# Queue order in a two-layer hybrid decoder trunk: first transfers on two queues, splits, exponentials and one value product moved

## The chip, the core and the metric

The kernel runs on one core of one Trainium2 chip. A core has five engines that work side by side, each through its own queue of instructions in order: TensorE (PE in the profile; PEld is its weight load), VectorE (DVE), ScalarE (ACT), GpSimd (POOL) and SyncE (SP, which here only issues transfers). The metric is the device time of one execution in microseconds (us); lower is better.

## The reference, cut to what matters

Two layers; x is 512 tokens by 1024, all in float32. Each layer is a half-step SwiGLU network, a mixer with three groups of heads, a second half-step SwiGLU network and a norm.

```python
for l in range(DEPTH):                                        # 2 layers
    h = x + 0.5 * swiglu(rms_norm(x, ffn1_norm[l]), ...)      # D 1024, FF 2816
    n = rms_norm(h, mix_norm[l])
    p = n @ w_in[l]
    u_conv, q, k, v, q_mem = jnp.split(p, splits, axis=-1)
    y_conv = conv_module(u_conv, ...)     # GLU, causal depthwise conv of 31 taps on 384 channels, LayerNorm, swish
    q = apply_rope(rms_norm(q.reshape(B, S, 6, 64), swa_q_norm[l]), cos, sin)
    k = apply_rope(rms_norm(k.reshape(B, S, 2, 64), swa_k_norm[l]), cos, sin)
    y_swa = sliding_window_attention(q, k, v, swa_sinks[l])   # window 128, softmax with a sink per head
    ...
    y_mem = memory_attention(qm, mk, mv)                      # 4 heads on 256 memory tokens
    y = jnp.concatenate([y_conv, y_swa, y_mem], axis=-1)
    h = h + y @ w_out[l]
    h = h + 0.5 * swiglu(rms_norm(h, ffn2_norm[l]), ...)
    x = rms_norm(h, final_norm[l])
```

## The kernel before, in words

The residual stream `h` lies transposed in SBUF as eight blocks d of 128 features by 512 tokens. Every float32 product is made of three passes (`mm3`, L176 to L178): each operand is split into a high and a low part, and high·high, low·high and high·low are added in PSUM. A split of a weight costs ACT one copy (`whi`, L145) and DVE one subtraction (`wlo`, L146). In `split_by_dma` ACT makes both halves (L150, L151), and a DMA that POOL issues adds the weight to the second (L152). `split_scaled` (L155, L156) makes `xhi` and `xlo`, the operand of the next stage, from a block of `h`; the same object adds the squares of the block to the sum for the next norm (`sq`, L236 on ACT; `st`, L248 on DVE), and PE sums that over features (L202).

At the start SP issues every transfer: the gains, half of w1, block 0 of x, half of w3, and the other blocks.

A network (`ffn`) makes its first products plainly and the rest with `up_pair`, a form with seven products in place of eight; each is followed by the products with w2. In the second layer's first network `after()` (L1053) rescales `h` by eight DVE instructions, issued behind the gate of the first `up_pair`.

The mixer follows a list of steps, `ORDER`: `c` is half a convolution projection, `q` queries and keys of one block of 128 tokens, `Q` their transposition, `v` values and memory queries of one block, `V` the transposition of the latter, `g` the scores of one group of heads, `a` attention, `t` taps, `s` the swish and what follows. `queries(0)` splits its four weights into the buffers `ghi` and `glo`. `attention` walks ten groups (`GROUPS`, `r` for memory, `w` for window): exponentials of the scores (L800, into `uu` or `pr`), transposition on PE (L810), copy on ACT (`aux`, L812), product with the values on PE (L821), division by the sums (`scaled`), transposition and split (`attended`). For window heads the sum has a term for the sink: POOL adds it (L791), ACT takes its exponential (`esw`, L829). The output weights are split in `out_weights`: two before the groups and one each at groups 3 and 5.

The 93 taps of the convolution (`taps`, L939) run on DVE as filler. `EARLY` of them are free; the others are tied by `LATER` to the groups: some so many behind each group's maxima (`nmr`, `nmw`).

A scheduler with a model of each engine turns the program into one fixed order per engine; `issue_after` names an instruction behind which another may be placed. It sets an order in the queue and no wait.

Of the kernel before, what the change touches and what calls it, by code (L numbers as in the profile page):

```python
# [13 lines left out]
AF = mybir.ActivationFunctionType  # L14
# [32 lines left out]
ORDER = "c00 c01 q0 c10 q1 c11 Q0 q2 q3 Q1 c20 c21 Q2 v0 v1 V0 Q3 V1 g0 g1 v2 v3 a t0 t1 t2 s"  # L47

EARLY = 49
LATER = (1, 12, 5, 4, 3, 3, 3, 3, 3, 3)  # L50
# [14 lines left out]
def trunk(ctx: ExitStack, tc: tile.TileContext, xT, memT, pos, w1a, w3a, w2a, w1b, w3b, w2b,  # L65
# [44 lines left out]
    nc.sync.dma_start(gn, gains)  # L110
# [4 lines left out]
    for k in range(KD):  # L115
        if k % 4 == 0:
            nc.sync.dma_start(first[0][:, halves[k // 4]], w1a[0, 0, :, halves[k // 4]])
        nc.sync.dma_start(h[:, k, :], xT[:, k, :])
        if k % 4 == 0:
            nc.sync.dma_start(first[1][:, halves[k // 4]], w3a[0, 0, :, halves[k // 4]])  # L120
# [33 lines left out]
    def split_scaled(hi, lo, x, col):  # L154
        A.activation(hi, x, AF.Copy, scale=col)  # L155
        V.scalar_tensor_tensor(out=lo, in0=x, scalar=col, in1=hi.bitcast(F32), op0=ALU.mult, op1=ALU.subtract)  # L156

# [95 lines left out]
    class Next:  # L253
# [5 lines left out]
        def __call__(self, d):  # L259
            split_scaled(self.x[0][:, d, :], self.x[1][:, d, :], h[:, d, :], self.gain[:, d : d + 1])  # L260
            for s, scale in self.stats:
                s.add(h[:, d, :], 1.0 if scale is None else scale[:, d : d + 1])
# [78 lines left out]
    def up_pair(l, w13, f, M):  # L341
# [26 lines left out]
        def add(out, a, b):  # L368
            V.tensor_tensor(out=out, in0=a, in1=b, op=ALU.add)  # L369
# [15 lines left out]
        for i in range(2):  # L385
            w = unit(X[i])
            product(xy[i][:, x0], w, 1, 5)
            A.activation(part[i][:, x0], xy[i][:, x0], AF.Copy)
            product(zv[i][:, x1], w, 0, 7)
            add(to[i][:, :, x1], zv[i].rearrange("p (n t) -> p n t", n=2), part[i][:, x0].unsqueeze(1).to_broadcast([P, 2, QT]))  # L390
# [14 lines left out]
    def ffn(l, w13, w2, x, sums, factors, last, at_product, aside=None):  # L405
# [44 lines left out]
        for q, (f0, nf) in enumerate(QUARTERS):  # L450
            ahead = 2 if q + 1 < len(QUARTERS) else 0
            for f in range(f0, f0 + nf + ahead, 2):
                if f not in g:
                    g[f], g[f + 1] = up_pair(l, w13, f, M)
                    if f == PLAIN:
                        with tc.issue_after(M.gated.ins):
                            after()
# [86 lines left out]

    def head_scale(ps, col, n, out=None):

        sq = tm("hsq", "sq", 2)[:, 0 : n * HD]
        A.activation(sq, ps, AF.Square, scale=col)
# [74 lines left out]
    def mixer(l, x, st, last):  # L623
# [28 lines left out]
        def spare():  # L652

            return tuple(z.rearrange("p i s -> p (i s)") for z in gated_pair())
# [38 lines left out]
        def queries(t):  # L693
            if not t:
                ww["q"] = [weights(wqk[l, i], 1024, G if i else V, spare()) for i in range(4)]
# [30 lines left out]
        def values(t):  # L726
# [9 lines left out]
            head_scale(ps[:, 0:256], rc[:, t : t + 1], NM, rm[:, t, :])  # L736

# [85 lines left out]
        def scaled(kind, b, po):  # L823
# [3 lines left out]
            if kind == "w":  # L827
                e = esw[:, b]
                A.activation(e, e, AF.Exp)  # L829
# [31 lines left out]
        def attention():  # L861
# [18 lines left out]
            for d in range(2):  # L880
                with tc.issue_after(keyed[2].ins):
                    out_weights(d)
            yy.extend([gated_pair() for _ in range(KD // 2)][::-1])
            y.extend(at(p, ALL, i, ALL) for p in yy for i in range(2))
            for n, (kind, *pairs) in enumerate(GROUPS):
# [8 lines left out]
                if n in (3, 5):  # L894
                    with tc.issue_after(raised[GROUPS[n - 1][0], *GROUPS[n - 1][-1]].ins):
                        out_weights(len(out_w))
# [108 lines left out]
    def stages(st, gain):  # L1005
        def factors(r):
            return gain, kept(spread(r), "R"), lambda: None

        return lambda: rms_cols(st, D), factors

    for l in range(L):
# [16 lines left out]
        mixer(l, nxt.x, before, into(gn[:, l, N_FFN2], (st, None)))  # L1028
        sums, factors = stages(st, gn[:, l, N_FFN2])
        st, fin = Stat("st"), gn[:, l, N_FIN]  # L1030
        if l + 1 < L:
# [15 lines left out]
            def factors(r, gg=gg, fin=fin):  # L1047
                R = kept(spread(r[1]), "R")

                def after():  # L1050
                    RF = kept(spread(r[0]), "RL")
                    for d in range(KD):
# [70 lines left out]
```

## Time and profile before

| what | value |
|---|---|
| median of 3 runs | 1791.13 us (1789.97 to 1793.52) |
| profiled execution | 1790.99 us, its span 1789.2 us |
| PE busy | 1757.0 us, 98% |
| DVE, ACT, POOL busy | 71%, 50%, 11% |
| PE idle inside the first 25 us | 6.4 us |
| PE busy from 25 to 300 us | 275 of 275 us |
| PE busy in 400 to 500 us and 1300 to 1400 us | 94.9 of 100 us each |

PE is busy nearly all the time, so the table is read from its few gaps: the start, the two mixers (about 355 to 530 us and 1237 to 1412 us) and the end. A granted clock below 1 in a stretch says that TensorE ran there at its lower level for a part of the time.

### The profile page before, as it was taken

The page shows a single profiled execution, that of the slowest core. Times are in us where ns is not written, and L with a number is a line of the kernel's source. Part 1 is how long each engine was busy: PE and PEld are TensorE (multiplying, and loading weights), DVE is VectorE, ACT ScalarE, POOL GpSimd, SP SyncE. Part 2 cuts the span into 40 slices and gives each one's busy share as a digit, 9 for nine tenths or more (in the row PEclk, how much of TensorE's full clock was granted, in tenths as well). Part 3 has the DMA queues.
Part 4 walks back from the last instruction along what each step waited for, and adds up shares of the span by engine and source line. Part 5 has one row for each costly group of instructions (what it writes and reads, how often), then busy time and mean ns, then how long its engine had stood idle before and what let it go on. Part 6 is the DMA issues. An engine that isn't in the chain of part 4 may idle for free.

```text
span 1789.2 us, 28081 instructions
## 1 busy us (share of the span) xinstructions
PE 1757.0 (98%) x11004; PEld 1581.5 (88%) x11004; DVE 1272.3 (71%) x1887; ACT 899.4 (50%) x1367; POOL 194.4 (11%) x217
## 2 busy tenths in 40 slices
PE   8999999999999999999999999999999999999997
PEld 6989999878788989898889898989787889998986
DVE  6969666589947857575678685756797567666755
ACT  6646444464765535353655453535455655453532
POOL 1001000034221000000010000000441210000000
PEclk9999999999999999999999999999999999999998
DMA  9456555183167547464656474643631966574622
GB/s 280 125 163 177 165 139 145 57 217 70 30 176 172 139 136 177 127 173 128 165 136 170 131 190 135 169 114 105 158 70 30 234 127 171 136 183 119 168 74 82
DMA packets 95892, 253.32 MB, mean 142 GB/s; under 512 B 9872, under 2 KB 14224, under 8 KB 95760
## 3 DMA queue, kind: packets, MB, share of 16 engines
q1 hardware_dynamic: 77040, 190.45, 34.9%
q0 software_dynamic: 18720, 61.09, 19.3%
q8 instruction: 86, 1.41, 0.3%
q14 instruction: 46, 0.38, 0.1%
HBM read 249.40 MB, written 2.10 MB: 141 GB/s over the span
## 4 chain that ended last, share of the span: by engine, by line
PE 81%; issue 6%; DVE 6%; DMA 4%; ACT 3%; POOL 0%; SPq 0%; POOLq 0%; DVEq 0%; ACTq 0%
PE mm L177 12%; PE mm L176 11%; PE mm L178 11%; PE po L176 8%; PE po L178 8%; PE po L177 8%; PE pt L176 6%; PE pt L177 6%; PE pt L178 6%; DVE there L939 2%; DMA glo<-in_wqk 1%; DMA raw<-in_wout 1%; DVE wlo L146 1%; PE cf L178 1%; PE cf L176 1%
## 5 line engine op out<-in xcount | busy, mean ns | idle before, releaser
L145 ACT ACTIVATE whi<-raw 128x1024 fp32r<-128x1024 f32 (+3 forms) x344 | 324.5, 945 | 440.5 <-PE mm L177 223.5
L146 DVE TENSOR_TENSOR wlo<-raw,whi 128x1024 fp32r<-128x1024 f32 (+3 forms) x344 | 372.0, 1083 | 133.9 <-ACT whi L145 132.6
L177 PE MATMUL mm<-glo,whi 128*128 128x512 f32 x752 | 293.3, 390 | 0.8 <-DVE glo L146 0.8
L176 PE MATMUL mm<-ghi,whi 128*128 128x512 f32 x752 | 293.3, 392 | 0.0
L178 PE MATMUL mm<-ghi,wlo 128*128 128x512 f32 x734 | 285.7, 389 | 0.9 <-DVE wlo L146 0.9
L177 PE MATMUL po<-ml,whi 128*128 128x256 f32 x864 | 244.5, 283 | 0.0
L178 PE MATMUL po<-mh,wlo 128*128 128x256 f32 x864 | 244.5, 283 | 0.0
L176 PE MATMUL po<-mh,whi 128*128 128x256 f32 x864 | 244.4, 283 | 0.0
L176 PE MATMUL pt<-xhi,whi 128*128 128x256 f32 x864 | 243.3, 283 | 0.6 <-DVE g L369 0.6
L178 PE MATMUL pt<-xhi,wlo 128*128 128x256 f32 x864 | 243.9, 283 | 0.0
L177 PE MATMUL pt<-xlo,whi 128*128 128x256 f32 x864 | 243.9, 283 | 0.0
L475 DVE SCALAR_TENSOR_TENSOR h<-mm,h 128x512 f32<-128x512 f32 x128 | 87.8, 689 | 133.3 <-PE mm L178 133.3
L177 PEld LDWEIGHTS mm<-glo,whi 128*128 128x128 f32 x752 | 141.3, 188 | 29.9 <-DVE glo L146 1.6
L176 PEld LDWEIGHTS mm<-ghi,whi 128*128 128x128 f32 x752 | 141.3, 188 | 29.4 <-DVE h L475 1.2
L176 PEld LDWEIGHTS pt<-xhi,whi 128*128 128x128 f32 x864 | 165.2, 192 | 1.7 <-DVE g L369 0.8
L177 PEld LDWEIGHTS pt<-xlo,whi 128*128 128x128 f32 x864 | 165.7, 192 | 0.8
L176 PEld LDWEIGHTS po<-mh,whi 128*128 128x128 f32 x864 | 165.8, 192 | 0.7
L177 PEld LDWEIGHTS po<-ml,whi 128*128 128x128 f32 x864 | 165.8, 192 | 0.6
L178 PEld LDWEIGHTS po<-mh,wlo 128*128 128x128 f32 x864 | 165.8, 192 | 0.0
L178 PEld LDWEIGHTS pt<-xhi,wlo 128*128 128x128 f32 x864 | 165.6, 192 | 0.0
L178 PEld LDWEIGHTS mm<-ghi,wlo 128*128 128x128 f32 x734 | 137.8, 188 | 30.2 <-DVE wlo L146 1.3
L939 DVE SCALAR_TENSOR_TENSOR there<-ypad,par,there 128x512 f32<-128x512 f32 x180 | 136.7, 770 | 1.6
(312 smaller groups left out, 3312.9 us busy)
## 6 DMA issues: line engine op xcount, KB each, us to landing
raw<-in_w2a SPq DMA_DIRECT2D x48, 384.0 KB, 3.5
raw<-in_w2b SPq DMA_DIRECT2D x48, 384.0 KB, 3.6
raw<-in_w1b SPq DMA_DIRECT2D x26, 512.0 KB, 3.7
raw<-in_w3b SPq DMA_DIRECT2D x26, 512.0 KB, 4.1
raw<-in_w1a SPq DMA_DIRECT2D x25, 512.0 KB, 3.7
raw<-in_w3a SPq DMA_DIRECT2D x25, 512.0 KB, 3.8
wsum<-in_w1a SPq DMA_DIRECT2D x18, 512.0 KB, 4.5
wsum<-in_w3a SPq DMA_DIRECT2D x18, 512.0 KB, 4.4
```

The source lines that it names most:

```text
L145: A.activation(hi, x, AF.Copy)
L146: on.tensor_tensor(out=lo, in0=x, in1=hi.bitcast(F32), op=ALU.subtract)
L176: T.matmul(ps, a[0], b[0], start=first, stop=False, **more)
L177: T.matmul(ps, a[0], b[1], start=False, stop=False, **more)
L178: tail[0] = T.matmul(ps, a[1], b[0], start=False, stop=last, **more)
L475: added = V.scalar_tensor_tensor(out=h[:, d, :], in0=ps, scalar=0.5, in1=h[:, d, :], op0=ALU.mult, op1=ALU.add)
L939: V.scalar_tensor_tensor(out=cv[:, c, :], in0=ypad[:, c, j : j + S], scalar=conv_w[:, c, j : j + 1], in1=cv[:, c, :], op0=ALU.mult, op1=AL ...
```

## The change

What it does, edit by edit. The gains and blocks 0 and 2 of x are loaded through ACT's queue, the rest through SP's. The splits of three of the four query weights are placed behind the last `xhi` of the stage before. The output weights 0 to 3 are split during `values` (three behind the first block's, one behind the third's) and no longer at the groups. The sinks' exponential is placed behind the last exponential of its block. In `ORDER` the value product `v2` stands in front of the first scores `g0`, and `g0` in front of `V1`. `EARLY` goes from 49 to 55 and `LATER` is shorter at its end. The rescaling of `h` is issued in two halves, behind the gates of two pairs.

```diff
-ORDER = "c00 c01 q0 c10 q1 c11 Q0 q2 q3 Q1 c20 c21 Q2 v0 v1 V0 Q3 V1 g0 g1 v2 v3 a t0 t1 t2 s"
-EARLY = 49
-LATER = (1, 12, 5, 4, 3, 3, 3, 3, 3, 3)
+ORDER = "c00 c01 q0 c10 q1 c11 Q0 q2 q3 Q1 c20 c21 Q2 v0 v1 V0 Q3 v2 g0 V1 g1 v3 a t0 t1 t2 s"
+EARLY = 55
+LATER = (1, 12, 5, 4, 3, 3, 3, 3, 2, 2)
...
-    nc.sync.dma_start(gn, gains)
+    nc.scalar.dma_start(gn, gains)
...
-        nc.sync.dma_start(h[:, k, :], xT[:, k, :])
+        (nc.scalar if k in (0, 2) else nc.sync).dma_start(h[:, k, :], xT[:, k, :])
...
-                    if f == PLAIN:
-                        with tc.issue_after(M.gated.ins):
-                            after()
+                    if f in (PLAIN, PLAIN + 2):
+                        with tc.issue_after((M.gated if f == PLAIN else M.turned).ins):
+                            after(f > PLAIN)
...
-                ww["q"] = [weights(wqk[l, i], 1024, G if i else V, spare()) for i in range(4)]
+                ww["q"] = []
+                for i in range(4):
+
+                    with tc.issue_after(operand.rounded.ins) if i else nullcontext():
+                        ww["q"].append(weights(wqk[l, i], 1024, G if i else V, spare()))
...
+            for d in {0: (0, 1, 2), 2: (3,)}.get(t, ()):
+                with tc.issue_after((squared[-1] if d > 1 else keyed[2]).ins):
+                    out_weights(d)
...
-                A.activation(e, e, AF.Exp)
+                with tc.issue_after(raised[kind, b, CC - 1].ins):
+                    A.activation(e, e, AF.Exp)
...
-            for d in range(2):
-                with tc.issue_after(keyed[2].ins):
-                    out_weights(d)
...
-                if n in (3, 5):
-                    with tc.issue_after(raised[GROUPS[n - 1][0], *GROUPS[n - 1][-1]].ins):
-                        out_weights(len(out_w))
...
+                def after(half):
+                    if not half:
+                        spreads.append(kept(spread(r[0]), "RL"))
+                    RF = spreads[0]
+                    for d in range(4 * half, 4 * half + 4):
```

The first place is ScalarE's queue at the first layer's mixer start; `xhi` are the last blocks of the operand, `sq` their squares, and each `ghi` with its `glo` the two halves of one query weight. Before:

```order
L155 ACTIVATE xhi_3587<-h_79,gn_80 128x512
L236 ACTIVATE sq_3689<-h_79 128x512
L150 ACTIVATE ghi_3847<-raw_3849 128x1024
L151 ACTIVATE glo_3848<-raw_3849 128x1024
L155 ACTIVATE xhi_3587<-h_79,gn_80 128x512
L236 ACTIVATE sq_3714<-h_79 128x512
L150 ACTIVATE ghi_3854<-raw_3856 128x1024
L151 ACTIVATE glo_3855<-raw_3856 128x1024
L155 ACTIVATE xhi_3587<-h_79,gn_80 128x512
L236 ACTIVATE sq_3739<-h_79 128x512
L150 ACTIVATE ghi_3861<-raw_3863 128x1024
```

The same place in the changed kernel, from the same `xhi` (block 5) on:

```order
L155 ACTIVATE xhi_3587<-h_79,gn_80 128x512
L237 ACTIVATE sq_3689<-h_79 128x512
L155 ACTIVATE xhi_3587<-h_79,gn_80 128x512
L237 ACTIVATE sq_3714<-h_79 128x512
L155 ACTIVATE xhi_3587<-h_79,gn_80 128x512
L150 ACTIVATE ghi_3847<-raw_3849 128x1024
L151 ACTIVATE glo_3848<-raw_3849 128x1024
L150 ACTIVATE ghi_3854<-raw_3856 128x1024
L151 ACTIVATE glo_3855<-raw_3856 128x1024
L237 ACTIVATE sq_3739<-h_79 128x512
L150 ACTIVATE ghi_3861<-raw_3863 128x1024
```

The last `xhi` has moved in front of two weights' halves; the last block's square, `sq_3739`, stands behind the same two weights as before.

The second place is ScalarE's queue around the first scores: `here`, `query` and `hsq` from a `po` tile are the reads of a value product, `there` from a `pt` tile is the copy of a transposition `V`, `whi` and `wlo` the halves of an output weight, `uu` the first exponentials. Before:

```order
L583 ACTIVATE there_3743<-pt_4281 128x2x128
L583 ACTIVATE here_3742<-pt_4285 128x3x128
L720 ACTIVATE here_3742<-pt_4285 128x128
L583 ACTIVATE there_3743<-pt_4292 128x2x128
L800 ACT_TABLE_LOAD
L800 ACTIVATE uu_3748<-mm_4296,nmr_3757,rm_3754 128x256
```

In the changed kernel:

```order
L586 ACTIVATE there_3743<-pt_4302 128x2x128
L586 ACTIVATE here_3742<-pt_4306 128x3x128
L728 ACTIVATE here_3742<-pt_4306 128x128
L741 ACTIVATE here_3742<-po_4313,rc_3752 128x2x64
L743 ACTIVATE query_3749<-po_4313,rc_3752 128x256
L551 ACTIVATE hsq_4340<-po_4313,rc_3752 128x256
L150 ACTIVATE whi_4347<-raw_4349 128x640
L151 ACTIVATE wlo_4348<-raw_4349 128x640
L586 ACTIVATE there_3743<-pt_4363 128x2x128
L812 ACT_TABLE_LOAD
L812 ACTIVATE uu_3748<-mm_4354,nmr_3757,rm_3754 128x256
```

Between the two copies `there` (of `V0` and of `V1`) now stand the three reads of `v2` and both halves of an output weight.

The third place is DVE's queue from the second value block's `hv` to the first window maxima; `there<-ypad,par,there` is a tap, `nmr` are the maxima of the memory scores, `nmw` those of the window scores. Before:

```order
L551 TENSOR_SCALAR hv_4277<-hs_4276 128x4
L939 SCALAR_TENSOR_TENSOR there<-ypad,par,there 128x512
L773 TENSOR_REDUCE nmr<-mm 128x2 x2
L774 SCALAR_TENSOR_TENSOR nmr<-nmr,rm 128x4
```

In the changed kernel:

```order
L554 TENSOR_SCALAR hv_4298<-hs_4297 128x4
L946 SCALAR_TENSOR_TENSOR there<-ypad,par,there 128x512 x5
L553 TENSOR_REDUCE hs_4342<-hsq 128x4
L785 TENSOR_REDUCE nmr<-mm 128x2 x2
L946 SCALAR_TENSOR_TENSOR there<-ypad,par,there 128x512
L554 TENSOR_SCALAR hv_4343<-hs_4342 128x4
L786 SCALAR_TENSOR_TENSOR nmr<-nmr,rm 128x4
```

From this `hv` to the instruction that finishes the first window maxima (`nmw<-nmw,nsink 128x6`) the queue has 14 taps before and 18 now; from the next `nmw<-nmw,nsink` to the last of the split parts `glo` before the final block it has 24 before and 22 now.

## Rows read from the trace of the kernel before

**Rows 1.** The page's first part: busy us, share of the span, instructions of each engine.

```profile
PE 1757.0 (98%) x11004; PEld 1581.5 (88%) x11004; DVE 1272.3 (71%) x1887; ACT 899.4 (50%) x1367; POOL 194.4 (11%) x217
```

**Rows 2.** PE's waits over the whole span: releaser, us in total, times, longest.

```profile
PE mm L176 <- ACT xhi L155: 7.5, 3, 6.3
PE po L821 <- ACT aux L812: 3.7, 2, 1.8
...
PE pt L581 <- ACT there L583: 1.6, 2, 0.8
...
PE mm L178 <- DVE wlo L146: 0.9, 1, 0.9
```

**Rows 3.** Timeline of ACT, start: start us, us, instruction, [idle before, releaser].

```profile
4.40 0.63 ACT L145 ACTIVATE whi<-raw 128x512 fp32r<-128x512 f32 x1 [2.17 <-DMA raw<-in_w1a]
5.53 0.72 ACT L155 ACTIVATE xhi<-h,gn 128x512 fp32r<-128x512 f32 x1 [0.50 <-DMA h<-in_xT]
```

**Rows 4.** Windows: stretch, length, busy of each engine, granted clock, DMA share, GB/s.

```profile
3.00:4.00 1.00, 0.00 (x0) 0.00 (x0) 0.00 (x0) 0.00 (x0) 0.00 (x0) 1.00 0.97 242
```

**Rows 5.** Timeline of ACT, first layer, mixer start.

```profile
371.21 1.06 ACT L150 ACTIVATE ghi<-raw 128x1024 fp32r<-128x1024 f32 x1
...
373.12 0.70 ACT L155 ACTIVATE xhi<-h,gn 128x512 fp32r<-128x512 f32 x1
373.73 0.62 ACT L236 ACTIVATE sq<-h 128x512 f32<-128x512 f32 x1
```

**Rows 6.** Timeline of DVE, the same place.

```profile
370.42 0.68 DVE L475 SCALAR_TENSOR_TENSOR h<-mm,h 128x512 f32<-128x512 f32 x1
...
374.53 0.68 DVE L248 TENSOR_TENSOR st<-st,sq 128x512 f32<-128x512 f32 x1
```

**Rows 7.** Timeline of PE, the same place.

```profile
375.27 1.05 PE L202 MATMUL cf<-onesq,st 128*128 128x1 f32 x8
```

**Rows 8.** Timeline of DVE, second layer, mixer start.

```profile
1252.56 0.68 DVE L475 SCALAR_TENSOR_TENSOR h<-mm,h 128x512 f32<-128x512 f32 x1
```

**Rows 9.** Timeline of PE, second layer, mixer start.

```profile
1257.65 1.05 PE L202 MATMUL cf<-onesq,st 128*128 128x1 f32 x8
```

**Rows 10.** Timeline of PE, first layer, from the second transposition V to attention.

```profile
438.04 0.44 PE L581 MATMUL pt<-cst,aux 128*128 128x128 f32 x2 [0.81 <-ACT there L583]
...
440.33 0.45 PE L176 MATMUL po<-ghi,xhi 128*128 128x384 f32 x1
...
448.79 0.60 PE L810 MATMUL pt<-cst,uu 128*128 128x128 f32 x4
```

**Rows 11.** Timeline of ACT, first layer, scores and first groups.

```profile
436.61 0.37 ACT L733 ACTIVATE here<-cf,rc 128x128 f32<-128x128 f32 x1 [3.01 <-PE cf L178]
...
437.59 0.39 ACT L583 ACTIVATE there<-pt 128x256 f32<-128x256 f32 x1
...
454.20 0.81 ACT L800 ACTIVATE uu<-mm,nmw,rq 128x128 f32<-128x128 f32 x2
...
457.44 0.73 ACT L150 ACTIVATE whi<-raw 128x640 fp32r<-128x640 f32 x1
458.07 0.59 ACT L812 ACTIVATE aux<-pt 128x512 f32<-128x512 f32 x1
```

**Rows 12.** Timeline of DVE, the same stretch.

```profile
443.19 3.90 DVE L939 SCALAR_TENSOR_TENSOR there<-ypad,par,there 128x512 f32<-128x512 f32 x5
...
454.00 0.17 DVE L790 TENSOR_TENSOR nmw<-nmw,nsink 128x6 f32<-128x6 f32 x1
```

**Rows 13.** Windows of 5 us with the clock below full, inside the two attentions.

```profile
460.00:465.00 5.00, 5.00 (x28) 3.46 (x27) 3.99 (x8) 2.50 (x8) 0.91 (x2) 0.66 0.74 131
...
1340.00:1345.00 5.00, 3.64 (x17) 3.65 (x18) 4.25 (x10) 4.32 (x11) 1.49 (x2) 0.64 0.41 76
1345.00:1350.00 5.00, 5.00 (x27) 3.37 (x27) 2.94 (x7) 1.43 (x4) 0.29 (x1) 0.68 0.31 55
```

**Rows 14.** Timeline of DVE, second layer's first network: the rescaling of h.

```profile
967.47 5.38 DVE L1053 SCALAR_TENSOR_TENSOR h<-h,gn,RL 128x512 f32<-128x512 f32 x8
```

More of the change, by code (lines that the diff above doesn't have):

```diff
@@ L154, in split_scaled @@
     def split_scaled(hi, lo, x, col):
-        A.activation(hi, x, AF.Copy, scale=col)
+        rounded = A.activation(hi, x, AF.Copy, scale=col)
         V.scalar_tensor_tensor(out=lo, in0=x, scalar=col, in1=hi.bitcast(F32), op0=ALU.mult, op1=ALU.subtract)
+        return rounded
     def pair():
@@ L259, in __call__ @@
         def __call__(self, d):
-            split_scaled(self.x[0][:, d, :], self.x[1][:, d, :], h[:, d, :], self.gain[:, d : d + 1])
+            self.rounded = split_scaled(self.x[0][:, d, :], self.x[1][:, d, :], h[:, d, :], self.gain[:, d : d + 1])
             for s, scale in self.stats:
@@ L368, in add @@
         def add(out, a, b):
-            V.tensor_tensor(out=out, in0=a, in1=b, op=ALU.add)
+            return V.tensor_tensor(out=out, in0=a, in1=b, op=ALU.add)
         for i in range(2):
@@ L389, in up_pair @@
             product(zv[i][:, x1], w, 0, 7)
-            add(to[i][:, :, x1], zv[i].rearrange("p (n t) -> p n t", n=2), part[i][:, x0].unsqueeze(1).to_broadcast([P, 2, QT]))
+            M.turned = add(to[i][:, :, x1], zv[i].rearrange("p (n t) -> p n t", n=2), part[i][:, x0].unsqueeze(1).to_broadcast([P, 2, QT]))
         w = unit(z)
@@ L543, in heads @@
         return x.rearrange("p (h e) -> p h e", e=HD)
+    squared = []
     def head_scale(ps, col, n, out=None):
         sq = tm("hsq", "sq", 2)[:, 0 : n * HD]
-        A.activation(sq, ps, AF.Square, scale=col)
+        squared.append(A.activation(sq, ps, AF.Square, scale=col))
         ss, v = sm(n, f"hs{n}"), sm(n, f"hv{n}")
@@ L621, in prepare, with mixer @@
         memory(l)
-    def mixer(l, x, st, last):
+    def mixer(l, operand, st, last):
+        x = operand.x
         o = CC * TAPS
@@ L1006, in factors @@
         def factors(r):
-            return gain, kept(spread(r), "R"), lambda: None
+            return gain, kept(spread(r), "R"), lambda half: None
         return lambda: rms_cols(st, D), factors
@@ L1027, in trunk @@
         before, st = st, Stat("st")
-        mixer(l, nxt.x, before, into(gn[:, l, N_FFN2], (st, None)))
+        mixer(l, nxt, before, into(gn[:, l, N_FFN2], (st, None)))
         sums, factors = stages(st, gn[:, l, N_FFN2])
@@ L1047, in factors @@
             def factors(r, gg=gg, fin=fin):
[L1048 to L1052, printed above, removed]
+                R, spreads = kept(spread(r[1]), "R"), []
+                def after(half):
[3 more added lines that the diff above has]
+                    for d in range(4 * half, 4 * half + 4):
                         V.scalar_tensor_tensor(out=h[:, d, :], in0=h[:, d, :], scalar=fin[:, d : d + 1], in1=RF, op0=ALU.mult, op1=ALU.mult)
```

## The prediction

> **What bounds the kernel now.** I read the page's first part before anything else: PE is busy for 1757.0 us of a span of 1789.2 [rows 1]. Two things can change the time, then: the 32.2 us in which PE stands, and the clock at which it runs. No edit takes a matmul away, so every term below is a stand of PE that is moved, lengthened or taken away, or a stretch of clock behind one.
>
> Next I read PE's waits [rows 2]. The reader is to see how small each is: 6.3 us for the first `xhi` of the kernel, two more waits for `xhi` that make 1.2 together (7.5 less 6.3; they stand at the two mixer starts), two of 1.8 for `aux` in attention, two of 0.8 for the copy behind a transposition, one of 0.9 for a `wlo`. The edits aim at all of these. Then I read the engines' timelines at those places, to see what the waited-for engine was doing, and last the windows with their granted clock [rows 13]: inside attention, behind the stands for `aux`, the mean clock of 5 us falls to 0.66 in layer 1, and to 0.64 and 0.68 in layer 2, which means TensorE spends much of these windows at 1.2 instead of 2.4 GHz. A window at 0.66 costs (1 − 0.66) × 5 = 1.7 us where PE is busy through it. That is my price for a fall of the clock.
>
> The sum is made against the profiled execution, 1790.99 us (span 1789.20 and 1.79 around it), 0.14 below the median of 1791.13. Its bound for no change is 0.2%, 3.6 us: faster is below 1787.5, slower above 1794.7.
>
> **The start: 0 (−0.7 to +0.9).** ACT splits the first weight at 4.40, waits, and begins `xhi` at 5.53 on the arrival of block 0 of x [rows 3]. The changed kernel sends block 0 through ACT's queue, beside the weights on SP's; but ACT's own order now has both weights' first copies ahead of the first `xhi`. The transfers are no idle resource there: at 3 to 4 us the DMA share is 0.97 at 242 GB/s [rows 4]. If the half of w3 and block 0 land close behind the first weight, `xhi` begins at 4.40 + 0.63 = 5.03 at best behind one copy, or 5.66 behind two less what they overlap: about 0.7 earlier than 5.53 at best. If the second weight lands only where `xhi` now stands, one copy of 0.63 and a small delay go in front of it: +0.9. I take 0, between the ends, as the load on the transfers is as large as before.
>
> The row of the DMA share is one place where the Trainium skill speaks against the edit: "Trainium Kernel Development and Optimization", section Key Constraints, says that transfers from SP's, ACT's and POOL's queues share the same 16 DMA engines, and that a second queue saves only issue time. The trace agrees so far as the share of 0.97 goes; by that rule this term would be at most the issue time, and the sum stays as it is.
>
> **The rescaling in halves: −1.05 (−1.1 to 0).** In layer 2's first network eight DVE instructions take 5.38 us in a row [rows 14], and a `wlo` that stands behind them holds PE for 0.9 [rows 2]. In halves only four stand there, 2.7 us, so the `wlo` comes 2.7 earlier, more than the 0.9 needed. I add 0.15 for the slower first matmul behind a wait. The second half must find 2.7 us on DVE one pair later, where DVE (71% busy over the span [rows 1]) waits for PE; without that room the 0.9 comes back there, hence the end at 0.
>
> **The mixer's start: +3.4 (0 to +4).** This is the term that I trust most. Before, ACT runs a weight's halves, `xhi`, `sq`, the next weight's halves, `xhi` and the last `sq`. The pair of halves takes 1.91 (371.21 to 373.12), `xhi` 0.61 to the next start, and the last `sq` begins at 373.73 [rows 5]; the last `st` follows on DVE at 374.53 [rows 6] and PE's sum over features at 375.27 [rows 7], 1.54 behind the start of `sq`. Now the last `xhi` goes ahead of two weights' halves, and the last `sq` still stands behind both. In layer 1 the last block of `h` is ready at 370.42 + 0.68 = 371.10 [rows 6]; `xhi` to 371.71, two pairs 3.82, so `sq` begins at 375.53 and the sum at 377.07 instead of 375.27: +1.80. In layer 2 `h` is ready at 1252.56 + 0.68 = 1253.24 [rows 8]; 1253.24 + 0.61 + 3.82 + 1.54 = 1259.21 instead of 1257.65 [rows 9]: +1.56. The waits of PE for `xhi` (1.2) go, but this gains nothing: PE takes its products earlier and then stands at the sum, which is next in its queue, for nearly 3 us at a time. The accumulating DMAs that POOL issues behind `glo` go out as much later, and PE wants them as much later: 0. The end at 0 is the case that the weights' halves run before `h` is ready and `sq` loses nothing.
>
> **The clock behind that stand: +1.7 (0 to +3.4).** No stand of this length away from the start is in the trace of before. The nearest, the 1.8 us for `aux` [rows 2], were both followed by windows at half clock [rows 13]. A stand of nearly 3 us may do the same once per layer, 1.7 each by the row above; I take one of two, since the stand here is in a stretch of dense products and not of short ones.
>
> **v2 ahead of the scores: +0.8 (−1.6 to +1.6).** The wait of 0.81 at the second transposition [rows 10] goes, twice. But its copy, which ran at 437.59 behind one read, now stands behind three reads of `v2` and an output weight's halves. `v2` and `v3` take 440.33 to 448.79 on PE, 4.23 each [rows 10]; put at 437.0, `v2` ends at 441.2. Its reads, 0.98 before the copy by 436.61 to 437.59 [rows 11], and the halves, 0.63 each as the pitch at 457.44 shows [rows 11], end near 443.6, and the copy at 444.0. The second scores `g1` could begin at 442.4 and stand 1.6. Set against the 0.81 that goes, and a little PE work to be shifted in, this leaves +0.4 per layer.
>
> **Attention's first groups: 0 (its ends are the rivals below).** From the second value block's `hv` to the end of the first window maxima DVE has 18 taps in place of 14. A run of five takes 3.90, 0.78 each [rows 12], so four more are 3.1 us; the new order also lets some of them fall into time in which DVE waits for ACT's squares, for which I take off 0.9. The maxima end at 454.00 + 0.17 now [rows 12] and would end 2.2 later; the window exponentials, 454.20 [rows 11], go to about 456.4. Three pairs of them follow, 0.7 each by the pitch of 454.20 to 457.44 less ACT's waiting, so the copy of the second window group, 458.07 [rows 11], begins near 458.5 although the weight's half at 457.44 is no longer in front of it. What the moved split gives, the taps take: the 1.8 us stand for `aux` stays.
>
> **Attention's end: −1.8 (−2.2 to −0.4).** Two of 24 taps and one weight's halves (2 × 0.63 = 1.26 of ACT) are gone from groups in which PE waits for ACT and DVE; the two make 1.26 + 2 × 0.78 = 2.8 per layer. I take a third of it, 0.9 per layer, since most of it lies beside PE's work.
>
> Sum: 0 − 1.05 + 3.4 + 1.7 + 0.8 + 0 − 1.8 = +3.05, so 1790.99 + 3.05 = 1794.0 us.
>
> **The rivals.** *Attention heals (faster).* If the window exponentials are not later than 454.2, `aux` comes in time, both stands go (3.7 [rows 2]) and with them the falls of the clock: 1.7, 1.8 and 1.6 by the three windows [rows 13], 5.1. With −1.05, +3.4 and +0.8 and no fall at the mixer's start: 1790.99 − 1.05 + 3.4 + 0.8 − 8.8 = 1785.3. For it: the weights' halves and the sink are out of ACT's way in front of the copy. Against it: four taps stand in front of the maxima. Chance 0.27.
>
> *The sum over features stands and the clock falls in both layers (slower).* The place is the mixer's start, the price 3.4 for the clock in place of the forecast's 1.7, and it decides as soon as PE's stand there is longer than the 1.8 us after which the clock fell before. With nothing gained at attention's end and the full 1.6 at v2: −1.05 + 3.4 + 3.4 + 1.6 = +7.35, 1798.3. For it: the only windows below full clock follow stands. Against it: the windows in question have short matmuls around them, these long ones. Chance 0.22.
>
> *The moves are hidden.* The delay at the mixer's start is taken back because attention's stands end on ACT's and DVE's work, which isn't delayed by PE: −1.05 and little else, 1790 to 1791. Against it: PE was busy all the way between. Chance 0.08.
>
> **How the numbers follow.** The forecast keeps 0.43, with its own range of 1790.5 to 1798. Faster by over 0.2% is nearly all of the first rival and a little of the forecast's tail, 0.28. Slower is nearly all of the second and the third of the forecast that lies above 1794.7, 0.33. The rest, 0.39, is within. The range goes from a little under the first rival to a little over the second: 1784.5 to 1799.5.
>
> **What would show it.** Right: in the profile after, PE waits at L202 for DVE's `st` at both mixer starts for 2.5 to 3 us, and ACT runs `sq` behind two pairs of `glo`; a wait of `g1` for ACT's copy stands where the 0.81 stood; the first window exponentials come over 1 us later relative to the first transposition of attention; no wait for `wlo` in layer 2's first network; the first matmul within 1 us of 6.3. Wrong: the sum over features less than 1 us later (the term of +3.4 falls), full clock in both attentions (the first rival), or clock below 1 in both mixer starts (the second).

## The result and the profile after

The changed kernel takes 1795.12 us (median of 20 runs, 1793.01 to 1797.36) against 1791.21 of the kernel before (20 runs): ratio 1.0021, 95% interval 1.0014 to 1.0027. The forecast was 1794.0. The change makes the kernel slower by 3.9 us; the bound of the prediction for no change, 0.2%, lies inside the interval. The profiled execution is 1795.92 us, its span 1794.1.

PE's waits over the whole span (releaser, us in total, times, longest), to be read against [rows 2]:

```profile
PE mm L177 <- ACT xhi L155: 7.6, 1, 7.6
PE cf L203 <- DVE st L249: 5.1, 2, 2.5
PE pt L822 <- ACT aux L824: 2.9, 4, 0.9
PE mm L781 <- ACT there L586: 2.6, 2, 1.3
PE po L833 <- ACT aux L824: 2.3, 2, 1.1
```

Most of the waits named in [rows 2] have changed. The first `xhi` comes 1.3 later, the two waits for it at the mixer starts are gone, and two waits of 2.5 for `st` stand there instead. The waits behind the transposition `V` have become 1.3 at the second scores (0.8 before), the two for `aux` 1.1 (1.8 before), and the `wlo` of 0.9 has gone.

ScalarE's timeline at the first mixer start (start us, us, instruction, [idle before, releaser]), which answers to [rows 5]:

```profile
371.49 0.73 ACT L155 ACTIVATE xhi<-h,gn 128x512 fp32r<-128x512 f32 x1 [2.38 <-DVE h L476]
372.12 0.62 ACT L237 ACTIVATE sq<-h 128x512 f32<-128x512 f32 x1
372.75 0.73 ACT L155 ACTIVATE xhi<-h,gn 128x512 fp32r<-128x512 f32 x1
373.38 1.05 ACT L150 ACTIVATE ghi<-raw 128x1024 fp32r<-128x1024 f32 x1
...
376.22 1.04 ACT L151 ACTIVATE glo<-raw 128x1024 fp32r<-128x1024 f32 x1
377.17 0.61 ACT L237 ACTIVATE sq<-h 128x512 f32<-128x512 f32 x1
```

The reader is to see two things. The last `sq` stands behind both pairs, 3.8 us behind its `xhi`. And ScalarE now stands idle for 2.38 in front of `xhi` of block 6, waiting for `h`: in the kernel before the first pair of halves filled that time, and `xhi` followed without a wait:

```profile
369.11 1.04 ACT L151 ACTIVATE glo<-raw 128x1024 fp32r<-128x1024 f32 x1
370.05 0.71 ACT L155 ACTIVATE xhi<-h,gn 128x512 fp32r<-128x512 f32 x1
```

PE, at the sum over features (answers to [rows 7] and [rows 9]):

```profile
378.56 1.61 PE L203 MATMUL cf<-onesq,st 128*128 128x1 f32 x8 [2.54 <-DVE st L249]
...
388.22 1.05 PE L216 MATMUL pt<-cst,rc 128*128 128x128 f32 x8
...
1265.05 1.05 PE L203 MATMUL cf<-onesq,st 128*128 128x1 f32 x8 [2.53 <-DVE st L249]
...
1273.10 1.05 PE L216 MATMUL pt<-cst,rc 128*128 128x128 f32 x8
```

L216 is the transposition of the norm's factors `rc`, which comes behind the same products in both kernels. In the kernel before, where [rows 7] has the sum, its line is L215:

```profile
381.71 1.05 PE L215 MATMUL pt<-cst,rc 128*128 128x128 f32 x8
```

From the sum to this transposition the first layer takes 9.66 us and the second 8.05; the kernel before took 6.44 (375.27 to 381.71). The windows (stretch, length, busy of PE, PEld, DVE, ACT, POOL, granted clock, DMA share, GB/s) say why:

```profile
375.00:380.00 5.00, 2.45 (x12) 1.74 (x11) 0.93 (x2) 5.00 (x7) 1.75 (x3) 0.89 0.65 143
380.00:385.00 5.00, 5.00 (x13) 3.94 (x14) 1.56 (x3) 1.91 (x2) 2.76 (x2) 0.50 1.01 253
385.00:390.00 5.00, 5.00 (x26) 4.25 (x25) 0.69 (x1) 0.00 (x0) 0.00 (x0) 0.93 1.07 277
1265.00:1270.00 5.00, 4.95 (x19) 4.10 (x20) 1.55 (x3) 3.40 (x4) 2.79 (x2) 0.66 0.99 221
```

TensorE ran at its lower level behind both stands: by these windows that costs 3.4 us in the first layer and 1.7 in the second. A third fall follows near 908 us (0.79 and 0.86 in the two windows from 905 to 915, 1.7 us), which the kernel before doesn't have in its profile. Inside both attentions, where [rows 13] show the clock below full, it is at 1.00 throughout. The stretch from the first transposition of attention to the next sum over features, both layers, before:

```profile
448.79:508.91 60.12, 55.79 (x385) 46.03 (x384) 49.24 (x107) 38.22 (x86) 10.41 (x12) 0.97 0.17 37
1331.43:1393.21 61.78, 57.45 (x385) 47.63 (x384) 49.28 (x107) 38.43 (x87) 10.44 (x12) 0.94 0.16 36
```

And in the changed kernel:

```profile
455.48:513.55 58.07, 54.71 (x385) 45.12 (x384) 46.00 (x105) 36.07 (x82) 8.00 (x9) 1.00 0.06 16
1340.90:1398.96 58.06, 54.73 (x385) 45.08 (x384) 46.06 (x105) 36.24 (x82) 8.00 (x9) 1.00 0.05 16
```

ScalarE in attention (answers to [rows 11]), and PE's stand:

```profile
461.88 0.81 ACT L812 ACTIVATE uu<-mm,nmw,rq 128x128 f32<-128x128 f32 x2 [1.07 <-DVE nmw L802]
...
463.26 0.82 ACT L812 ACTIVATE uu<-mm,nmw,rq 128x128 f32<-128x128 f32 x2
463.94 0.23 ACT L842 ACTIVATE esw<-esw 128x6 f32<-128x6 f32 x1
464.04 0.89 ACT L824 ACTIVATE aux<-pt 128x512 f32<-128x512 f32 x2
```

```profile
455.48 0.60 PE L822 MATMUL pt<-cst,uu 128*128 128x128 f32 x4
...
464.71 1.11 PE L833 MATMUL po<-mvn,aux 128*128 128x65 f32 x8 [1.15 <-ACT aux L824]
```

Against the first transposition of attention (448.79 before, 455.48 now) the window exponentials come 1.0 later (6.40 instead of 5.41), as the taps had it, but the copy `aux` comes 0.7 earlier (8.56 instead of 9.28): between the last exponentials and it there is only `esw`, 0.1 by the pitch, and no half of a split any more.

The start, ScalarE's timeline (answers to [rows 3]):

```profile
4.41 0.63 ACT L145 ACTIVATE whi<-raw 128x512 fp32r<-128x512 f32 x1 [0.76 <-DMA raw<-in_w1a]
5.93 0.63 ACT L145 ACTIVATE whi<-raw 128x512 fp32r<-128x512 f32 x1 [0.90 <-DMA raw<-in_w3a]
6.86 0.72 ACT L155 ACTIVATE xhi<-h,gn 128x512 fp32r<-128x512 f32 x1 [0.30 <-DMA h<-in_xT]
```

Block 0 now lands behind the half of w3 and is used 1.3 later than before, although its transfer is issued 0.5 earlier (at 1.18 from ScalarE's queue, before at 1.65 from SyncE's); the half of w3 is issued beside it, at 1.19 (2.12 before). The first matmul is at 7.64 instead of 6.30.

How much of this is left further on differs between profiles. Of the first 25 matmuls of the program, those of over 0.5 us number 14 in the changed kernel and 6 in `no_q`, an experiment below with the same start. The changed kernel, then `no_q`:

```profile
12.49 0.63 PE L179 MATMUL mm<-xhi,wlo 128*128 128x512 f32 x1
```

```profile
12.43 0.39 PE L179 MATMUL mm<-xhi,wlo 128*128 128x512 f32 x1
```

The first sum over features, at 19.82 in the kernel before, is at 21.45 in the changed kernel and at 19.91 in `no_q`.

### The profile page after: what moved, and what is told of

Read it like the earlier page. It is cut to its first block, busy times and chain, and to the rows that moved or that the text cites. A ratio compares the mean times of both kernels' runs of the same rounds, so it can differ in the third digit from the quotient of the medians.

```text
span 1794.1 us, 28077 instructions
## 1 busy us (share of the span) xinstructions
PE 1759.2 (98%) x11004; PEld 1582.7 (88%) x11004; DVE 1267.6 (71%) x1887; ACT 900.1 (50%) x1367; POOL 196.6 (11%) x217
## 4 chain that ended last, share of the span: by engine, by line
PE 83%; DVE 7%; issue 6%; DMA 3%; ACT 2%; SPq 0%; POOLq 0%; POOL 0%; DVEq 0%; ACTq 0%
PE mm L177 12%; PE mm L178 12%; PE mm L179 12%; PE po L177 8%; PE po L179 8%; PE po L178 8%; PE pt L177 6%; PE pt L178 6%; PE pt L179 6%; DVE there L946 3%; PE cf L177 1%; PE cf L179 1%; PE cf L178 1%; DVE nmw L800 1%; DVE wlo L146 1%
```

## The experiments

Theory A of the first experiments: the query weights' placement makes the stands, and the stands drop the clock; attention gains. The rival B: the falls of the clock come for another reason. Each kernel was timed beside the kernel before on one chip; the ratios are to it, and 0.001 of a ratio is 1.8 us. The mean granted clock over the runs of a kernel stands with most: 0.001 of it is 1.8 us of span where PE is busy. It counts the end of the program too (0.64 from 1774 to 1789 us in the kernel before), where PE is busy for only 4.5 of the 15 us and a low clock costs little, so a difference of 0.0005 says nothing.

**Changed kernel without the query weights' placement** (`no_q`):

```diff
-                    with tc.issue_after(operand.rounded.ins) if i else nullcontext():
+                    with nullcontext():
```

> The changed kernel with one edit undone: the query weights' splits are placed as before, so ACT runs the last square behind one weight's halves again and not two. Theory A: the edit makes PE stand 2.5 us before the sum over features in each mixer, and that stand drops TensorE's clock behind it; by the changed kernel's trace the sum comes 1.7 and 1.1 later by it and the clock costs 3.2 and 1.6 more, 7.6 in all. Expected: about 1787.5 us (1795.1 less 7.6), no wait of PE for st, granted clock 1.0 in both mixer starts. Theory B: the falls of the clock there come for another reason, and only the two shifts go: about 1792.3, with a clock below 1 behind the sum still. Theory C: PE takes the delay back later in attention, and nothing is gained: 1794 to 1796.

1788.85 us, ratio 0.9994 (0.9985 to 1.0002), 12 runs, mean clock 0.9952 (0.9938 with the edit). No wait for `st`, and clock 1.00 in both mixer starts of the profile, which is of the fastest of the twelve runs. The edit costs 1.0021 − 0.9994, some 4.8 us (about 2 either way by the two intervals), less than A's 7.6 and more than B's 2.8. C falls.

**The placement alone** (`q_alone`), the same edit put into the kernel before:

> The kernel before with one edit: the splits of three query weights placed behind the last xhi. Theory A: the same 7.6 us the other way, about 1798.8, two waits for st of about 2.5 us at the sums over features and a clock near 0.5 in the windows behind them. Theory B: 1794, the shifts alone, full clock. Theory C: 1790 to 1792.

1795.95 us, ratio 1.0038 (1.0025 to 1.0051), 6 runs, mean clock 0.9918 (0.9941 before). By the ratio this is +6.8, near A's 7.6 and far from B and C. PE's sum in the first layer and four windows:

```profile
376.96 1.87 PE L203 MATMUL cf<-onesq,st 128*128 128x1 f32 x8 [2.53 <-DVE st L249]
```

```profile
380.00:385.00 5.00, 5.00 (x16) 3.90 (x16) 0.45 (x2) 0.32 (x1) 1.17 (x1) 0.64 1.05 283
905.00:910.00 5.00, 5.00 (x18) 4.07 (x18) 0.66 (x4) 1.68 (x2) 3.36 (x4) 0.66 0.84 205
1265.00:1270.00 5.00, 5.00 (x14) 4.03 (x15) 1.56 (x3) 2.28 (x3) 2.79 (x2) 0.50 1.01 244
460.00:465.00 5.00, 3.17 (x28) 2.93 (x28) 4.96 (x11) 4.07 (x11) 2.19 (x4) 1.00 0.05 20
```

The sum is 1.7 later than in the kernel before, and both mixers lose clock. But there is also a fall at 905, behind a wait of PE of 0.26, and none in attention behind the same 1.8 us stands as before: a stand alone doesn't decide where the clock falls.

**The stand filled** (`filled`):

```diff
+                if i == 0:
+                    spill = bank([P, S], "pt")
+                    for _ in range(11):
+                        with queued():
+                            tail[0] = T.matmul(spill, w[0][:, 0:P], x[0][:, 0, :], start=True, stop=True)
```

> The changed kernel with eleven matmuls of 512 columns whose result nobody reads in front of the sum over features of each mixer, 2.5 us of PE work in the place of the stand. Theory A (the stand drops the clock): the sum comes at the same time as in the changed kernel, the granted clock stays at 1.0 behind it, and 3.2 + 1.6 = 4.8 us are saved: about 1790.3. Theory B (the clock falls for another reason, the narrow matmuls of the sum for one): the clock falls as before, 1795.

1796.25 us, ratio 1.0034 (1.0022 to 1.0045), 8 runs, mean clock 0.9955. At its place A holds in the profile:

```profile
375.92 2.67 PE L676 MATMUL pt<-xhi,whi 128*128 128x512 f32 x11
378.62 1.05 PE L203 MATMUL cf<-onesq,st 128*128 128x1 f32 x8
...
385.08 1.05 PE L216 MATMUL pt<-cst,rc 128*128 128x128 f32 x8
```

The sum is where it was (378.56), the clock stays at 1.00 and L216 comes 3.1 earlier; in layer 2 it is 1.7 (1271.44 against 1273.10). The time isn't less. In layer 1 the profile shows PE giving it back: with some 1.0 more waiting for the DMAs of `glo`, 1.9 of the 3.1 is left at the first transposition of attention (453.54 against 455.48), and with a clock of 0.87 and 0.79 at 460 to 470 nothing is left at the sum near 553 us (553.19 against 553.24). Behind that PE waits 1.0 more for `g` (L370). There is no fall near 908 here, and the span of the profile is 0.4 shorter than the changed kernel's. So in this profile the fall at its own place goes with the stand, but the saving of 4.8 that A expected did not come. Over the runs the mean clock is 0.0017 above the changed kernel's, some 3 us, and the time is no lower: what takes this back is open.

**Splits behind the last square** (`sq_first`):

```diff
-                    with tc.issue_after(operand.rounded.ins) if i else nullcontext():
+                    with tc.issue_after(operand.squared.ins) if i else nullcontext():
```

> The changed kernel with the splits placed behind the last square in place of the last xhi: xhi stays early, and the square no longer stands behind two weights' halves. Theory A: PE finds st ready as soon as its products are done, no stand before the sum, full clock, and the waits of the kernel before for the last xhi and xlo (0.74 and 0.98) are gone too: 1795.1 less 7.6 less 1.7, about 1785.8. Theory B: the clock still falls and it gains 2.8 + 1.7 = 4.5: about 1790.6. Against both: the accumulating DMAs of the splits go out 0.6 later; if PE then waits for a glo, up to 1 us is lost again.

1796.05 us, ratio 1.0032 (1.002 to 1.0044), 5 runs, mean clock 0.9958: ten us off A. The sum has no wait for `st`, but the query product waits for its weights. PE's waits, and GpSimd's timeline:

```profile
PE mm L178 <- DMA glo<-in_wqk: 8.5, 4, 2.5
```

```profile
375.23 0.86 POOL L152 DMA_DIRECT2D glo<-in_wqk  x1 [36.57 <-ACT glo L151]
376.33 1.03 POOL L194 TENSOR_TENSOR rsq<-ms,nhalf 128x4 f32<-128x4 f32 x1 [0.24 <-DVE ms L209]
377.34 0.91 POOL L152 DMA_DIRECT2D glo<-in_wqk  x1
379.02 0.86 POOL L152 DMA_DIRECT2D glo<-in_wqk  x1 [0.77 <-ACT glo L151]
```

The accumulating DMAs go out late, the last two behind `rsq`, land 7.4 to 12.7 us after issue, and PE, no longer late itself, reaches the product first. In the changed kernel they go out no earlier (375.7 to 380.0) and PE waits 0.2 for them: the stand at the sum and the slow stretch behind it cover this. I had put this risk at 1 us; it was 8.5. In layer 1 the clock stayed at 1.00 behind these waits of 2.5 and 2.2.

**The start alone** (`start_alone`), the kernel before with `nc.scalar` for the gains and blocks 0 and 2:

> The kernel before with one edit: the gains and blocks 0 and 2 of x on ACT's queue. Theory A: block 0 no longer has the transfers to itself in front of the half of w3, ACT splits both weights before the first xhi, and the first matmul comes at about 7.6 us instead of 6.3; PE carries 1.3 to 1.6 us of that to the end: about 1.4 slower than the kernel before. Theory B: PE waits less later in the first 20 us and the sum over features at 19.8 comes at the same time: no change.

1792.69 us, ratio 1.0003 (0.9994 to 1.0013), 12 runs. The first matmul is at 7.63 and the sum of the first mixer at 377.10 instead of 375.27, so the profile, of the slowest of the twelve runs, carries the delay. The timing alone, +0.5 us (−1.1 to +2.3), tells it neither from none nor from A's 1.4.

**Attention's edits alone** (`attention_alone`: `ORDER`, `EARLY`, `LATER`, output splits, sinks):

> The kernel before with the edits in front of and inside attention alone: the order of v2, g0 and V1, the output weights' splits, the sinks' exponentials, and the taps. Theory A: the stand for aux shrinks from 1.83 to 1.15 in each layer and the clock no longer falls behind it: 1.9 saved in layer 1 and 3.2 in layer 2, 5 us in all: about 1786. Theory B: the clock's falls come by chance; only the shorter waits count, 0.7 at aux and some 0.8 later in attention less 0.5 at the second scores, 1.0 per layer: about 1789. In the trace of A there is no window below 1 in either attention.

1788.82 us, ratio 0.9988 (0.998 to 0.9997), 12 runs, mean clock 0.9952 (0.9942 before). The stand is 1.14, as A has it, but the profile has clock falls near 376, 902 and 1342 all the same, the last inside attention, right behind a stand of 1.15. The time is B's. The mean clock is 0.0010 higher than before, 1.8 us, so how much of the −2.1 is shorter waits and how much is clock stays open.

**Sinks' exponential back** (`sink_back`):

```diff
-                with tc.issue_after(raised[kind, b, CC - 1].ins):
-                    A.activation(e, e, AF.Exp)
+                A.activation(e, e, AF.Exp)
```

> The same as attention_alone, but with the sinks' exponentials back where they were in ScalarE's queue, in front of the third pair of window exponentials. Theory A: ScalarE waits for GpSimd's sum of the sinks there again (0.94 in the kernel before), the copy for the second window group comes that much later, and PE's stand for aux grows from 1.15 to about 2 us, with the clock falling behind it: 1 to 4 us slower than attention_alone. Theory B: GpSimd has its sum ready earlier in this order and the place in the queue costs nothing: the same as attention_alone within 1 us, the stand 1.2.

1789.32 us, ratio 0.9988 (0.9979 to 0.9996), 12 runs: the same. The wait of 0.94 doesn't come back, since GpSimd has its sum (`esw`) ready before its part of the convolution (`aux`):

```profile
456.08 0.65 POOL L803 TENSOR_TENSOR esw<-nmw,rw 128x6 f32<-128x6 f32 x1
457.73 1.26 POOL L951 TENSOR_TENSOR aux<-there 128x512 f32<-128x512 f32 x1 [1.01 <-DVE there L945]
```

The kernel before had them the other way round:

```profile
454.73 1.27 POOL L945 TENSOR_TENSOR aux<-there 128x512 f32<-128x512 f32 x1
455.96 0.65 POOL L791 TENSOR_TENSOR esw<-nmw,rw 128x6 f32<-128x6 f32 x1
```

**Output splits back at the groups** (`splits_back`), the rest of attention changed:

```diff
-            for d in {0: (0, 1, 2), 2: (3,)}.get(t, ()):
...
+                if n in (3, 5):
+                    with tc.issue_after(raised[GROUPS[n - 1][0], *GROUPS[n - 1][-1]].ins):
+                        out_weights(len(out_w))
```

> attention_alone with the output weights' splits back at the groups. Theory A: the half of a split that ScalarE runs in front of the copy for the second window group (0.63) is back, and PE's stand for aux grows from 1.14 by as much, to about 1.8 as in the kernel before; the first two splits are out of the way of the second scores, so the wait of 1.28 there falls to 0.6 or less. Time about that of attention_alone, 1789 to 1790, unless the clock falls more often. Theory B: the stand shrank because GpSimd's sum of the sinks no longer stands behind its part of the convolution, which comes with the taps and stays: the stand stays near 1.2.

1796.0 us, ratio 1.003 (1.0017 to 1.0043), 7 runs, mean clock 0.9914. ScalarE and PE:

```profile
458.12 0.76 ACT L150 ACTIVATE whi<-raw 128x640 fp32r<-128x640 f32 x1
458.75 0.62 ACT L821 ACTIVATE aux<-pt 128x512 f32<-128x512 f32 x1
```

```profile
459.42 1.11 PE L830 MATMUL po<-mvn,aux 128*128 128x65 f32 x8 [2.04 <-ACT aux L821]
```

The stand grows by 0.9, a little more than the half split's 0.63, and 7.5 us are lost by the ratios: without the moved splits the rest of attention's edits doesn't pay. Most of the loss is clock: the mean is 0.9952 in `attention_alone` and 0.9914 here, some 6.8 us, and the profile has the clock below full behind both stands of 2.04 (PE's total idle time is even 0.7 less than in the kernel before's profile). A was right on the stand and far off on the time.

**Tap numbers back** (`taps_back`, 49 and the old list):

> attention_alone with the old numbers for the taps (49 free, the old list by groups). Theory A: DVE has fewer taps in front of the first window maxima, the window exponentials start earlier by up to 1 us against the first transposition, and PE's stand for aux shrinks further, to between 0.2 and 0.8; the taps come back at the end of attention, where waits for aux of some 0.5 grow again. Time within 1 us of attention_alone. Theory B: with the old numbers GpSimd's part of the convolution stands in front of its sum of the sinks again, but the exponential is no longer in front of the window exponentials, so only the division by the sums comes later: the stand stays 1.14.

1792.4 us, ratio 1.0012 (1.0003 to 1.002), 11 runs. The stand in front of the product with the values has gone, but the transpositions wait instead:

```profile
PE pt L822 <- ACT aux L824: 8.6, 10, 1.6
```

Both theories miss: the taps are worth 4.3 us by the ratios, and PE's waits in the two attentions are 3.7 longer in the profile. B misses in its mechanism too: with the old numbers GpSimd still has its sum of the sinks first (454.98, its part of the convolution at 462.01).

**Queries and start undone** (`no_q_start`; attention and halves are left):

> The changed kernel with two edits undone, the query weights' placement and the first transfers; what is left is attention and the rescaling in halves. By the sum of the parts: attention_alone less the 0.9 of the wait for wlo, about 1787.9; by the changed kernel without the query edit alone, less the 1.4 at the first matmul: 1787.5.

1787.24 us, ratio 0.9979 (0.997 to 0.9988), 9 runs, mean clock 0.9964. Against `no_q` this puts the start at 0.9994 − 0.9979, 2.7 us (0.5 to 4.9 by the two intervals); against `attention_alone` the halves at 1.6 with 0.9 expected, but the two intervals overlap, and the time alone doesn't tell this from nothing.

**One DMA split early, two behind the square** (`pair_free`, on the base of `no_q_start`):

```diff
-                    with nullcontext():
+                    with tc.issue_after(operand.squared.ins) if i > 1 else nullcontext():
```

> The kernel before with the edits at attention and the rescaling in halves, the first transfers on one queue, and the query weights placed anew: the first split by DMA free (so that it fills ScalarE's wait for the last but one block), the two others behind the last square. Theory A: the last xhi and square come 2 us earlier than in the kernel before, PE's waits of 0.74 and 0.98 there go, and the first accumulating DMA still goes out early: about 1.5 less than the changed kernel without the query edit and with the old start, some 1785.5. Theory B: what is gained is lost again when PE reaches the query product, because the second and third DMA go out 1.2 and more later and land 8 to 12 us after that: 1787 to 1790, with a wait for the DMA of glo of over 1 us in each layer.

1788.36 us, ratio 0.9981 (0.9972 to 0.999), 12 runs: B. No wait at the sum, waits for the DMA of 1.56 and 2.07.

**The last two query weights split by VectorE** (`q_dve`):

```diff
-ww["q"].append(weights(wqk[l, i], 1024, G if i else V, spare()))
+ww["q"].append(weights(wqk[l, i], 1024, G if i == 1 else V, spare()))
```

> pair_free with two of its three accumulating DMAs gone: the third and fourth query weight are split by ScalarE and VectorE, as the first is. Theory A: the DMA's 8 to 12 us to landing is what PE waited for at the query product (1.56 and 2.07); VectorE stands idle for 6 us behind the sum over features and has the two subtractions of 1.2 done in time: both waits go, 3.6 us less than pair_free less what other waits take back: about 1785.5, in any case under 1787.5. Theory B: VectorE's subtractions come in front of the product of the norm with the first convolution half and delay it, and PE waits there or at the transposition of the queries: the same as pair_free or slower.

1784.77 us, ratio 0.996 (0.9947 to 0.9973), 5 runs: 0.7 below A. No wait of PE for a DMA is left, nor for the last `xhi`; VectorE does both subtractions behind the last `st`, where it was mostly idle:

```profile
375.00 2.38 DVE L146 TENSOR_TENSOR glo<-raw,ghi 128x1024 fp32r<-128x1024 f32 x2
```

The row `ms` behind them, which leads to the factors `rc`, comes 2.8 later than in `pair_free` (378.80 against 376.02), and PE doesn't feel it, which was B's fear. By the ratio this version is 7.2 us faster than the kernel before (5.6 by the medians of its chip), and about 10 faster than the changed one; of the kernels here it is the fastest.

## Why the prediction was right, point by point

The forecast of 1794.0 came within 1.1 us, on the side that it named, and its main term, the late square in the mixer's start, is shown. But the nearness is partly luck: other terms were wrong and made up for each other. By the prediction's own list, two of the three signs of being wrong came true in the profile (full clock in both attentions, clock below 1 at both mixer starts), and of the signs of being right the first matmul, 7.64, is not within 1 us of 6.3.

- **The mixer's start (+3.4): right in mechanism and nearly in size.** `sq` behind both pairs, the sum waiting for `st`, PE standing: all as written. The sum came 1.7 later in layer 1 by `q_alone` (1.80 forecast). In layer 2 it was about 1.0 against 1.56: the changed kernel's sum is 7.40 late (1265.05 against 1257.65), of which some 6.4 come from before it (5.56 at the sums near 905, 905.54 against 899.98, and 1.7 from the fall of the clock behind those, less the 0.89 of the `wlo`). In `q_alone` it is 1.3 by the same reckoning (6.29, less 3.28 and 1.7). What I hadn't seen is where the time is lost: the first pair had filled ScalarE's wait for `h`, which is now idle. That the DMAs of `glo` go out later and cost nothing was right (0.2 of waiting).
- **The clock behind it (+1.7): mis-sized.** The profile lost 3.2 and 1.6; over the runs the mean clock puts what the query edit costs in clock between 2.5 us (0.9952 less 0.9938, times the span) and 4.1 us (0.9941 less 0.9918). I had counted one fall out of two, and the first cost twice the price. Yet the net is near the forecast by another road: the profile's three falls cost 6.8, and the falls of [rows 13], which were to stay, are gone with their 5.1, which leaves 1.7. Over the runs the net is under 1 us (mean clock 0.9938 against 0.9941 to 0.9943 of the kernel before).
- **The start (0, −0.7 to +0.9): mis-sized, above its own upper end.** The first matmul came at 7.55 to 7.78 in the five profiles with this edit and at 5.90 to 6.30 in the nine without. At the first sum over features, near 20 us, the five stand at 19.91 to 21.54 and the nine at 19.26 to 20.09, by their means 1.2 apart. By the times it is +0.5 (`start_alone`) or +2.7 (`no_q` against `no_q_start`), each to about 2 either way, so the times can't size it closer. I allowed for one more copy in front of `xhi`; block 0 itself came 1.3 later though issued earlier, and the transfers beside it, both weights, are the likely cause: the DMA share was 0.97 in [rows 4], and by it I should have placed the term at the upper end. The Trainium skill's rule of the shared DMA engines ("Trainium Kernel Development and Optimization", section Key Constraints) rightly left no room for a gain: the earlier issue on a second queue brought block 0 no earlier.
- **v2 ahead of the scores (+0.8): right.** The wait went from 0.81 to 1.27, 0.46 a layer.
- **Attention's first groups (0): failed.** "The 1.8 us stand for `aux` stays" was wrong; it fell to 1.14. The step that failed is the exponentials: they came 1.0 later and not 2.2, for PE was 0.7 later itself and four taps took 1.7 of the 2.2 that I gave them. ScalarE's part was right, 2.16 from the exponentials to the copy (2.1 forecast), but it took for granted that the 0.94 of the wait on GpSimd's `esw` goes. It goes with the order of GpSimd's two instructions; `sink_back` shows that the place of the exponential is not needed for it, and `taps_back` that the numbers of taps are not. Which edit turns the order is open.
- **Attention's end (−1.8): not shown, by the profile smaller.** From the first transposition to the next sum over features layer 1 gained 2.05 (60.12 to 58.07) and layer 2 3.72 (61.78 to 58.06), 5.8 in all. Of this, 5.1 are the falls of [rows 13] that the changed kernel's profile doesn't have there. PE's idle time in the two stretches fell by 2.0 (60.12 less 55.79 and 61.78 less 57.45, against 58.07 less 54.71 and 58.06 less 54.73), of which 1.4 are the two shorter stands for `aux`; some 0.6 is left for the end. About 1.3 went the other way, in PE's busy time, and is not explained. By `attention_alone`, all of it with v2 is −2.1 (−3.6 to −0.5); the three terms gave −1.0, inside that interval.
- **The rescaling (−1.05): right in the profile.** The `wlo` of 0.9 is gone; the times are too coarse to size it.

Put together from the kernels that have one edit each: queries +6.8 (`q_alone`), start +0.5 (`start_alone`), attention −2.1 (`attention_alone`), and −0.9 for the `wlo` by the profile make +4.3 against 3.9 measured. Each of the three ratios is good to 1.5 to 2.3 us either way, so this is agreement within the noise. (Taken off the changed kernel one after the other, the edits give +4.8, +2.7 and −3.8; these add up to the whole by construction and test nothing.) So the query weights' placement is what makes the kernel slower, by 4.8 to 6.8, and attention's edits take part of it back. The rival "attention heals" was half true (no fall of the clock there in the changed kernel's profile, the stands only shorter; but `attention_alone`, `filled` and `q_dve` have a fall there behind stands of 1.15 to 1.17, so this is partly chance), and the rival of the clock falling in both layers was true; held apart they lay 13 us from each other, together they met near the forecast.

Open: what decides where the clock falls. Stands of 2.5 at the sum were followed by a fall all four times (changed kernel and `q_alone`), the one of 2.5 for a DMA in layer 1 of `sq_first` was not; all fourteen profiles wait 0.25 to 0.26 near 900 to 910 us, and seven have a fall behind it; and in `filled` the falls at the sums went and one came elsewhere. One profile does not show what a kernel loses to the clock on average. The Trainium skill, "TensorE: Matmul & The Clock Gate", section Part 1, says that how many matmuls run slow at a kernel's start varies from run to run. The profiles agree: the four kernels with the changed kernel's start (`no_q`, `sq_first`, `filled` and itself) have 6, 8, 13 and 14 of the first 25 over 0.5 us.

## What to carry to other kernels

Before moving work behind an instruction, ask what idle time it filled: here a pair of splits that cost nothing in ScalarE's wait became, with a second pair, 3.8 us in front of a square that PE waits for. A late engine also hides late transfers, so taking a stand away shows the next wait behind it (8.5 us in `sq_first`), and of the three kernels that took the stand away by another placement (`sq_first`, `pair_free`, `q_dve`) only `q_dve`, which took both waits away, gained on its kernel without the placement (0.9960 against 0.9979 of `no_q_start`, the intervals hardly overlapping). Where several terms carry chances, add the likely falls of the clock as well as the stands, and take a loaded queue's term from its bad end.

## What was not expected of the hardware

An accumulating DMA of half a megabyte, issued by GpSimd, took 7.4 to 12.7 us from issue to landing in `sq_first`; in the kernel before such DMAs took 8.5 to 10.7, and the plain transfers of the same weights, the same size, 3.6 in the median. One `tensor_tensor` of 4 columns (1.03 us) stood between two of them in GpSimd's queue. The gains, 40 KB, took 3.8 us to land from ScalarE's queue beside the other transfers, and 1.7 from SyncE's ahead of them.
